# Adding a causal mask to attention scores: on VectorE in 32-bit floats, or as a bf16 product on TensorE

## The chip, the cores and the metric

The kernel runs on one core of one Trainium2 chip. The metric is the device time in microseconds of one execution. Five engines work side by side, each through its own queue in order: TensorE (PE in the profile, its weight loads PEld), VectorE (DVE), ScalarE (ACT), GpSimd (POOL) and SyncE (SP), which here issues the DMAs. TensorE writes its products to PSUM, which VectorE and ScalarE can read and write.

## The reference, cut to what matters

One decoder block over 1040 tokens (16 learned meta tokens ahead of 1024), model width 1024, all in 32-bit floats. After a norm and one input projection, 8 heads of 64 channels attend, beside a gated short convolution of 512 channels; both are normed by head, projected back, and a squared-ReLU MLP of width 4096 and a last norm follow. The attention adds a decay to the scores and masks the future:

```
s = einsum('bqhd,bkhd->bhqk', q_block, k) * scale
s = where(causal, s + cum[q] - cum[k], -1e30)
p = softmax(s);  out = einsum('bhqk,bkhd->bqhd', p, v)
```

A block of 128 queries sees 16 + 128 (i + 1) keys (i = 0 to 7); only the last 128 of them need the mask, a triangle.

## The kernel before

Products keep the precision of 32-bit floats by splitting each operand into a rounded part (type fp32r) and the rest: a ScalarE copy makes the first (`split`, L116), a VectorE or GpSimd subtract the second (`low`, L113), and three products are summed.

From about 111 us to 510 us the attention runs, as 64 slots: 8 heads of 8 query blocks (L696 to L739). A slot's work on its critical path is: `scores` (L513) writes 128 queries by 144 to 1040 keys into one PSUM tile `S` of three banks (one buffer), in one to three chunks, two products a chunk (L527, L528); behind the last chunk comes one more product, of an identity in bf16 with a bf16 mask of 0 and -1e30 (L530), onto the last 128 columns (132 for the longest block). VectorE takes the negated maximum of the rows (L533, `nm`), ScalarE the exponential with its sum (L537, `pr`). One slot later `transposed` (L541) turns `pr` by TensorE (L550) and splits it (`pth`, `ptl`, L116 and L113); behind every second slot `weighted` (L558) multiplies it with the values (L564 to L566).

What is independent of this fills TensorE's time. `fill` (L692) draws products from one list, so many nominal microseconds a slot (`QUOTA0`, then `QUOTA1`, four fifths of it behind the scores): first the rest of the input projections (`project`, L465), and from about 397 us, when these are used up, the convolution's half of the output projection (`out_conv`, L655). The latter loads its rows and weights through two buffers named `raw` (L589, L605), whose DMAs are ordered with TensorE's instructions, splits them (`yh`, `wa`, `wc`) and adds the result to the residual `h` (L669).

The order of TensorE's instructions in the attention is the order of the program (`pe`, L104). The other engines' queues are laid out by a planner, which estimates durations and takes what is ready, by priority; a queue once laid out is fixed. In the first part and after 514 us, most instructions of every engine are held in program order (`pin`, L109).

After the attention come the rest of the output projection with a norm (L851), and from about 592 us the two MLP products (L979, L1284), which TensorE works through with hardly a hole.

At the start (L80 to L89) GpSimd makes the identity `ident` in 32-bit floats, VectorE casts it to `identb`, and GpSimd makes `maskb` with a memset and a select.

Of the kernel before, what the change touches and what calls it, by code (L numbers as in the profile page):

```python
# [10 lines left out]

F32 = mybir.dt.float32
F32R = mybir.dt.float32r
BF16 = mybir.dt.bfloat16
AF = mybir.ActivationFunctionType
ALU = mybir.AluOpType
AX = mybir.AxisListType
# [3 lines left out]
P = 128  # L21
EPS = 1e-5
NEG = -1e30
# [18 lines left out]
def hymba_block(  # L42
# [5 lines left out]
    nc = tc.nc  # L48
# [6 lines left out]
    HD = 64  # L55
# [11 lines left out]
    KPAD = 4  # L67
# [6 lines left out]
        name=nc.get_next_instruction_name(), act_func_set_id=LN_EXP_SET, ins=[], outs=[]))  # L74

    const = ctx.enter_context(tc.tile_pool(name="const", bufs=1))
# [2 lines left out]

    ident = const.tile([P, P], F32, name="ident")  # L80
    make_identity(nc, ident)
    identb = const.tile([P, P], BF16, name="identb")
    nc.vector.tensor_copy(identb, ident)
    maskb = const.tile([P, P + KPAD], BF16, name="maskb")
    nc.gpsimd.memset(maskb, 0.0)
    nc.gpsimd.affine_select(
        out=maskb, in_=maskb, compare_op=ALU.is_ge, fill=NEG, base=0,
        pattern=[[-1, P + KPAD]], channel_multiplier=1,
    )  # L89
    bones = const.tile([P, P], F32R, name="bones")  # L90
# [13 lines left out]
    def pe(ins):  # L104
        return tc.keep_in_program_order(ins) if ORDERED[0] else ins
# [53 lines left out]
    def bank(tag):  # L159
        return pp.tile([P, 512], F32, name=tag, tag=tag, bufs=BANKS[tag])  # L160
# [140 lines left out]
    for g in range(0, NK, 4):  # L301
        ps = bank("tr")[:NH]
        w = 0
# [111 lines left out]
    def conv_groups(ct):  # L415
        st = {}
        p0 = NM - 2
        ch = chunks(p0, T + 2, 3)

        def evac_c(ps, t0, n):  # L420
            if not st:
                st["cu"] = page(st)
            nc.scalar.copy(st["cu"][:, t0 - p0:t0 - p0 + n], ps)

        def evac_u(ps, t0, n):
            cu = st["cu"][:, t0 - p0:t0 - p0 + n]
            nc.vector.tensor_tensor(out=cu, in0=ps, in1=cu, op=ALU.mult)

        def taps():
            cu = st["cu"]  # L430
            st["y"] = yc = page(st)[:, :T]
            nc.vector.tensor_scalar(yc, cu[:, 0:T], cw[:, 0, ct:ct + 1], None, op0=ALU.mult)
            for j in (1, 2):
                nc.vector.scalar_tensor_tensor(
                    out=yc, in0=cu[:, j:j + T], scalar=cw[:, j, ct:ct + 1], in1=yc, op0=ALU.mult, op1=ALU.add)

        def evac_b(ps, t0, n):
            s = st["y"][:, t0 - NM:t0 - NM + n]
            nc.vector.tensor_tensor(out=s, in0=ps, in1=s, op=ALU.mult)

        def norm():
            (a, b), (c, d) = head_norm(st["y"], NP + ct, 0), head_norm(st["y"], NP + ct, 1)

            def middle():
                b()
                c()

            pending.extend([a, middle, d])

        return [(CC + ct * P, ch, evac_c, None), (CU + ct * P, ch, evac_u, taps),  # L450
                (CB + ct * P, chunks(NM, T, 2), evac_b, norm)]
# [61 lines left out]
    def scores(i, st, s):  # L513

        qa, qb, ka, kb = st
        n = NM + P * (i + 1)
        nb = 2 * (i // 2) + 2
        qs = slice(i * P, (i + 1) * P)
        nch = -(-n // 512)
        pad = -n % (2 * nch)  # L520
        v = (n + pad) // nch
        w = max(v, 256)
        ps = pp.tile([P, 3, 512], F32, name="S", bufs=BANKS["S"])
        for c in range(nch):
            ks = slice(c * v, c * v + w)
            last = c == nch - 1
            pe(nc.tensor.matmul(ps[:, c, :w], qa[:, qs], ka[:, ks], start=True, stop=False))  # L527
            pe(nc.tensor.matmul(ps[:, c, :w], qb[:HD + 4, qs], kb[:HD + 4, ks], start=False, stop=not last))  # L528
            if last:
                pe(nc.tensor.matmul(ps[:, c, v - P - pad:v], identb, maskb[:, :P + pad], start=False, stop=True))  # L530
        ps = ps[:, :nch, :v]
        nm = small.tile([P, 1], F32, name="nm")
        nc.vector.tensor_reduce(nm, ps, axis=AX.XY, op=ALU.max, negate=True)  # L533
        pr = at.tile([P, L + KPAD], F32, name="pr", bufs=3)
        if n < nb * P:
            nc.gpsimd.memset(pr[:, n:nb * P], 0.0)
        nc.scalar.activation(  # L537
            pr[:, :n + pad].rearrange("p (a b) -> p a b", b=v), ps, AF.Exp, bias=nm, accum_out=s)
        return pr
# [137 lines left out]
    c = [conv_groups(ct) for ct in range(NC)]  # L677
# [22 lines left out]
    ORDERED[0] = True  # L700
    fill(START)
    pr = scores(0, st[0], sums[0][:, 0, 0:1])
    late = None
    for t, (h, i) in enumerate(slots):
# [8 lines left out]
        if t + 1 < len(slots):  # L713
            h1, i1 = slots[t + 1]
            p1, j1 = divmod(h1, 2)
            if p1 not in o:
                o[p1] = at.tile([P, T], F32, name="opair", bufs=2)
                sums[p1] = at.tile([P, NT, 2], F32, name="sums", bufs=2)
            pr = scores(i1, st[h1], sums[p1][:, i1, j1:j1 + 1])
# [588 lines left out]
    v = [vp.tile([P, HD2], F32, name=f"v{tt}") for tt in range(NH2)]  # L1308
# [136 lines left out]
```

## Time and profile before

| | |
|---|---|
| median of 3 runs | 1193.27 us (1193.04 to 1193.37) |
| the profiled execution | 1195.17 us, its span 1193.4 us |
| busy in the span, VectorE | 727.7 us (61%), 989 instructions |
| busy in the span, ScalarE | 544.5 us (46%), 911 instructions |
| busy in the span, GpSimd | 212.5 us (18%), 211 instructions |
| mean granted TensorE clock | 0.992 of full speed |
| chain that ended last, TensorE's share | 87% |

The span runs from the first instruction to the last; the execution's time is that and some 1.8 us around it. The profiled execution is one of its own and lies 1.9 us above the median. Matmul records overlap, since products are pipelined: what a product costs is read from starts, not from its duration. Idle time of an engine that doesn't set the end costs nothing.

### The profile page before, as it was taken

To read this page: it belongs to the slowest core of one execution; us is meant where nothing else is said; L and a number is where in the kernel's file an instruction comes from. 1 tells how busy PE (TensorE), PEld (TensorE's weight loads), DVE (VectorE), ACT (ScalarE), POOL (GpSimd) and SP (SyncE) were. 2 spreads that over 40 slices of the span, in tenths; PEclk is the share of its full clock that TensorE was granted. 3 is DMA by queue.
4 is the path that set the end of the run, shared out by engine and by line. 5 is a ranking of instruction groups with operands and counts; after the bars stand their busy time and mean duration, and the time that the engine had idled before them with its cause. 6 is when DMAs were issued, how large, how long until landed. Compare 5 with 4: busy or idle time off the path is not lost.

```text
span 1193.4 us, 15645 instructions
## 1 busy us (share of the span) xinstructions
PE 1155.6 (97%) x5969; PEld 982.8 (82%) x5969; DVE 727.7 (61%) x989; ACT 544.5 (46%) x911; POOL 212.5 (18%) x211
## 2 busy tenths in 40 slices
PE   6999999999999899998899999999999999999997
PEld 6988989899888677886788888888888888888886
DVE  7632354444454556659778866666665546985687
ACT  6522335453455555546444353444544433333444
POOL 3011123222221121201523431323100000000000
PEclk9999999999999899999999999999999999999999
DMA  8448241543332564265345445354479866522561
GB/s 249 148 140 246 72 89 41 144 136 77 80 105 77 193 172 159 98 212 175 107 133 194 159 133 193 109 183 140 152 248 344 289 201 222 159 89 71 185 238 71
DMA packets 120123, 185.92 MB, mean 156 GB/s; under 512 B 9552, under 2 KB 61776, under 8 KB 120048
## 3 DMA queue, kind: packets, MB, share of 16 engines
q1 hardware_dynamic: 120048, 184.92, 48.7%
q8 instruction: 47, 0.77, 0.3%
q14 instruction: 28, 0.23, 0.1%
HBM read 126.30 MB, written 58.59 MB: 155 GB/s over the span
## 4 chain that ended last, share of the span: by engine, by line
PE 87%; DVE 5%; DMA 3%; ACT 3%; issue 2%; DVEq 0%; ACTq 0%; SPq 0%
PE acc L1284 26%; PE acc L979 24%; PE mm L465 18%; PE tr L550 3%; PE mm L655 2%; PE wide L851 2%; PE mm L251 2%; PE S L251 1%; PE pv L564 1%; PE pv L565 1%; PE S L527 1%; PE S L528 1%; DMA raw<-y_conv 1%; DMA raw<-in_w_out_dram 1%; PE pv L566 1%
## 5 line engine op out<-in xcount | busy, mean ns | idle before, releaser
L1284 PE MATMUL acc<-w2h,a2l 128*128 128x512 f32 x440 | 171.2, 389 | 0.0
L1284 PE MATMUL acc<-w2h,a2h 128*128 128x512 f32 x440 | 171.2, 389 | 0.0
L1284 PE MATMUL acc<-w2l,a2h 128*128 128x512 f32 x440 | 171.2, 389 | 0.0
L465 PE MATMUL mm<-xh,wh 128*128 128x342 f32 (+3 forms) x416 | 145.0, 349 | 1.0 <-DVE vm L260 0.8
L465 PE MATMUL mm<-xh,wl 128*128 128x342 f32 (+3 forms) x416 | 144.8, 348 | 0.0
L465 PE MATMUL mm<-xl,wh 128*128 128x342 f32 (+3 forms) x416 | 144.7, 348 | 0.0
L116 ACT CAST a2h<-ar 128x1024 fp32r<-128x1024 f32 x54 | 56.8, 1052 | 147.5 <-PE acc L1284 83.2
L113 DVE TENSOR_TENSOR a2l<-ar,a2h 128x1024 fp32r<-128x1024 f32 x54 | 66.1, 1224 | 86.1 <-ACT a2h L116 86.1
L1284 PEld LDWEIGHTS acc<-w2h,a2l 128*128 128x128 f32 x440 | 82.6, 188 | 17.3
L1284 PEld LDWEIGHTS acc<-w2l,a2h 128*128 128x128 f32 x440 | 82.6, 188 | 17.2
L1284 PEld LDWEIGHTS acc<-w2h,a2h 128*128 128x128 f32 x440 | 82.6, 188 | 17.0
L465 PEld LDWEIGHTS mm<-xh,wh 128*128 128x128 f32 x416 | 78.5, 189 | 7.8 <-DVE vm L260 1.1
L465 PEld LDWEIGHTS mm<-xh,wl 128*128 128x128 f32 x416 | 78.5, 189 | 6.1
L465 PEld LDWEIGHTS mm<-xl,wh 128*128 128x128 f32 x416 | 78.6, 189 | 6.0
L113 DVE TENSOR_TENSOR ptl<-tr,pth 128x512 fp32r<-128x512 f32 (+1 forms) x96 | 56.1, 596 | 38.3 <-ACT pth L116 37.7
L113 POOL TENSOR_TENSOR wl<-wr,wh 128x512 fp32r<-128x512 f32 x40 | 53.4, 1355 | 116.0 <-ACT wh L116 99.1
L786 ACT ACTIVATE ac<-ac 128x1024 f32<-128x1024 f32 (+1 forms) x64 | 66.5, 1041 | 13.0 <-DVE ac L780 11.8
L537 ACT ACTIVATE pr<-S,nm 128x144 f32<-128x144 f32 (+3 forms) x64 | 48.5, 757 | 46.4 <-DVE nm L533 46.0
L116 ACT CAST pth<-tr 128x512 fp32r<-128x512 f32 (+1 forms) x96 | 47.7, 514 | 43.7 <-PE tr L550 31.4
L533 DVE TENSOR_REDUCE nm<-S 128x1 f32<-128x144 f32 (+3 forms) x64 | 49.3, 771 | 24.6 <-PE S L530 24.1
L780 DVE TENSOR_TENSOR ac<-acc,cv 128x512 f32<-128x512 f32 x61 | 41.7, 687 | 28.6 <-PE acc L979 28.4
L116 ACT CAST ws12h<-w1s 128x1024 fp32r<-128x1024 f32 x16 | 16.9, 1055 | 87.5 <-PE acc L979 84.3
(275 smaller groups left out, 2678.8 us busy)
## 6 DMA issues: line engine op xcount, KB each, us to landing
ar<-a_scr SPq DMA_DIRECT2D x54, 512.0 KB
w1r<-in_w_ff_dram SPq DMA_DIRECT2D x16, 1024.0 KB
a_scr<-ac SPq DMA_DIRECT2D x16, 1024.0 KB
a_scr<-sm SPq DMA_DIRECT2D x16, 768.0 KB
w<-in_w_ff_dram SPq DMA_DIRECT2D x24, 512.0 KB
wr<-in_w_in_dram SPq DMA_DIRECT2D x40, 256.0 KB
w2r<-in_w_ff_dram SPq DMA_DIRECT2D x16, 512.0 KB
k_scr<-pg SPq DMA_DIRECT2D x8, 520.0 KB
```

The source lines that it names most:

```text
L113: pin((eng or nc.vector).tensor_tensor(out=lo, in0=src, in1=r32(hi), op=ALU.subtract))
L116: pin(nc.scalar.copy(hi, src))
L251: pin(nc.tensor.matmul(ps[half], lhs, w_[:, k, f0:f0 + fn], start=k == 0 and a == 0, stop=k == KD - 1 and a == len(terms) - 1))
L465: pe(nc.tensor.matmul(ps, x_[:, k], y_[:, k, ts], start=k == 0 and a == 0, stop=k == KD - 1 and a == 2))
L533: nc.vector.tensor_reduce(nm, ps, axis=AX.XY, op=ALU.max, negate=True)
L537: nc.scalar.activation(pr[:, :n + pad].rearrange("p (a b) -> p a b", b=v), ps, AF.Exp, bias=nm, accum_out=s)
L550: pe(nc.tensor.transpose(ps[:, jj], pr[:, kt * P:(kt + 1) * P], ident))
L655: pe(nc.tensor.matmul(ps, y_[:, k], w_[:, cs], start=k == 0 and a == 0, stop=k == NC - 1 and a == 2))
L780: pin(eng.tensor_tensor(out=out, in0=a, in1=b, op=ALU.add))
L786: pin(nc.scalar.activation(out, src, func, **more))
L979: pe(nc.tensor.matmul(ps, w[w_][:, k], m[m_][:, k], start=k == a == 0, stop=k == HK - 1 and a == 2))
L1284: pe(nc.tensor.matmul(banks[tt], w[w_][:, k, tt * P:(tt + 1) * P], m[m_][:, k], start=first and f == k == a == 0, stop=last and f == len(f ...
```

## The change

The bf16 identity and mask go, and the mask is kept in 32-bit floats. In `scores`, the last chunk's second product ends the accumulation like the others, the third product is gone, and VectorE adds the mask to the last 128 (or 132) columns in PSUM, in place, before the maximum.

```diff
-    identb = const.tile([P, P], BF16, name="identb")
-    nc.vector.tensor_copy(identb, ident)
-    maskb = const.tile([P, P + KPAD], BF16, name="maskb")
-    nc.gpsimd.memset(maskb, 0.0)
+    mask = const.tile([P, P + KPAD], F32, name="mask")
+    nc.gpsimd.memset(mask, 0.0)
     nc.gpsimd.affine_select(
-        out=maskb, in_=maskb, compare_op=ALU.is_ge, fill=NEG, base=0,
+        out=mask, in_=mask, compare_op=ALU.is_ge, fill=NEG, base=0,
         pattern=[[-1, P + KPAD]], channel_multiplier=1,
     )
...
         for c in range(nch):
             ks = slice(c * v, c * v + w)
-            last = c == nch - 1
             pe(nc.tensor.matmul(ps[:, c, :w], qa[:, qs], ka[:, ks], start=True, stop=False))
-            pe(nc.tensor.matmul(ps[:, c, :w], qb[:HD + 4, qs], kb[:HD + 4, ks], start=False, stop=not last))
-            if last:
-                pe(nc.tensor.matmul(ps[:, c, v - P - pad:v], identb, maskb[:, :P + pad], start=False, stop=True))
+            pe(nc.tensor.matmul(ps[:, c, :w], qb[:HD + 4, qs], kb[:HD + 4, ks], start=False, stop=True))
+        end = ps[:, nch - 1, v - P - pad:v]
+        nc.vector.tensor_tensor(out=end, in0=end, in1=mask[:, :P + pad], op=ALU.add)
         ps = ps[:, :nch, :v]
```

## Rows read from the trace of the kernel before

**Rows 1.** The page, busy time: engine, us, share of the span, instructions.
```profile
PE 1155.6 (97%) x5969; PEld 982.8 (82%) x5969; DVE 727.7 (61%) x989; ACT 544.5 (46%) x911; POOL 212.5 (18%) x211
...
```

**Rows 2.** Stretches: us, engines' busy us (instructions), TensorE's clock, DMA share, GB/s.
```profile
111.00:397.00 286.00, 283.99 (x1740) 255.59 (x1739) 124.94 (x204) 131.47 (x288) 66.23 (x81) 1.00 0.35 98
397.00:467.00 70.00, 60.15 (x334) 47.21 (x333) 44.17 (x72) 41.24 (x88) 14.09 (x20) 0.95 0.59 177
467.00:514.00 47.00, 47.00 (x266) 38.82 (x267) 25.88 (x47) 23.34 (x53) 8.72 (x10) 0.96 0.38 125
...
592.00:1150.00 558.00, 558.00 (x2463) 462.05 (x2462) 378.72 (x408) 237.66 (x261) 86.17 (x60) 1.00 0.54 181
```

**Rows 3.** Weight loads' waits, 111-396, then 396-515 us: total us, times, longest.
```profile
PEld tr L550 <- ACT pr L537: 1.6, 2, 1.3
...
PEld tr L550 <- ACT pr L537: 9.5, 8, 2.6
```

**Rows 4.** Chain that ended last, 396 to 468 us: start, us, what.
```profile
414.14 0.89 DVE nm L533
...
430.20 4.85 DMA raw<-in_w_out_dram
...
435.73 1.30 DVE wa L113
...
451.81 0.46 DVE nm L533
```

**Rows 5.** Mask products in 113-397, 398-467, 467-515 us: durations, first and last start.
```profile
L530 PE MATMUL S<-maskb,identb x42: 230/231/233, 113.4 to 396.5; 128*128 128x128 bf16 x37, 128*128 128x132 bf16 x5
...
L530 PE MATMUL S<-maskb,identb x13: 230/231/233, 399.1 to 461.8; 128*128 128x128 bf16 x11, 128*128 128x132 bf16 x2
...
L530 PE MATMUL S<-maskb,identb x8: 230/231/232, 468.2 to 498.6; 128*128 128x128 bf16 x7, 128*128 128x132 bf16 x1
```

**Rows 6.** TensorE in order of time around one mask: start us, us, instruction.
```profile
241.11 0.31 PE L527 MATMUL S<-ka,qa 128*128 128x328 f32 x1
241.26 0.31 PE L528 MATMUL S<-kb,qb 68*128 68x328 f32 x1
241.41 0.23 PE L530 MATMUL S<-maskb,identb 128*128 128x128 bf16 x1
241.45 0.48 PE L465 MATMUL mm<-xh,wl 128*128 128x512 f32 x1
241.77 0.39 PE L465 MATMUL mm<-xh,wh 128*128 128x512 f32 x1
242.00 0.39 PE L465 MATMUL mm<-xl,wh 128*128 128x512 f32 x1
```

**Rows 7.** VectorE by shape (busy, mean ns, idle before), then tile S (min/median/max ns).
```profile
L113 DVE TENSOR_TENSOR ptl<-tr,pth 128x512 fp32r<-128x512 f32 x64 | 43.8, 687 | 38.2 <-ACT pth L116 37.7
...
L113 DVE TENSOR_TENSOR tail<-tr,tail 16x128 fp32r<-16x128 f32 x32 | 9.0, 280 | 32.4 <-ACT tail L116 32.1
...
L113 DVE TENSOR_TENSOR vt<-S,vt 128x256 fp32r<-128x256 f32 x8 | 3.4, 421 | 11.0 <-ACT vt L116 11.0
...
L263 DVE TENSOR_TENSOR zt<-S,bfb x4: 153/156/156, 32.5 to 68.6; 128x8 f32<-128x8 f32 x4
```

**Rows 8.** VectorE in order of time: a dependent pair, then an independent one.
```profile
6.16 0.22 DVE L121 SCALAR_TENSOR_TENSOR rs_t<-rs_r,rs_v 128x1 f32<-128x1 f32 x1 [0.41 <-ACT rs_r L131]
6.41 0.16 DVE L122 SCALAR_TENSOR_TENSOR rs_t<-rs_t,rs_r 128x1 f32<-128x1 f32 x1
...
241.02 0.75 DVE L370 SCALAR_TENSOR_TENSOR n_y<-pg,og,n_sq 128x512 f32<-128x512 f32 x1 [1.23 <-ACT n_sq L368]
...
241.69 0.83 DVE L533 TENSOR_REDUCE nm<-S 128x1 f32<-128x656 f32 x1
```

**Rows 9.** VectorE in order of time at the start; in brackets its idle time before.
```profile
2.35 0.96 DVE L83 CAST identb<-ident 128x128 bf16<-128x128 f32 x1
...
5.59 0.15 DVE L130 TENSOR_SCALAR rs_v<-ss 128x1 f32<-128x1 f32 x1 [2.29 <-ACT xn L210]
```

More of the change, by code (lines that the diff above doesn't have):

```diff
@@ L13 @@
 F32R = mybir.dt.float32r
-BF16 = mybir.dt.bfloat16
 AF = mybir.ActivationFunctionType
```

## The prediction

> **What bounds the kernel now.** I read the page first: TensorE is busy for 1155.6 us of a span of 1193.4 us [rows 1], so the question is where its 37.8 idle us lie and where a saved product is saved time. Busy time by stretch answers that [rows 2]. From 111 to 397 us, where scores alternate with the projections that fill TensorE's time, TensorE is busy for 284.0 of 286 us with the granted clock at 1.00: this stretch is as long as TensorE's list of products. From 397 to 467 us, where the filler has become the output projection, it is busy for only 60.2 of 70 us and the clock's mean is 0.95. From 467 to 514 us the records cover the stretch again. From 592 to 1150 us TensorE is busy all the time, and the planner's freedom is small there, so what the attention gains or loses reaches the end of the kernel.
>
> The waits come next, because the change lengthens one path: scores, maximum (VectorE), exponential (ScalarE), transposes (TensorE). In the first stretch TensorE's weight load for the transposes waits for the exponential only 2 times, 1.6 us in all; from 396 us on it waits 8 times, 9.5 us in all [rows 3]. So the path has slack nearly everywhere before 396 us and little behind it. The chain of waits shows what sets the time behind it: a ring of loads into the two `raw` buffers, a DMA (4.85 us in the row), a ScalarE cast, VectorE subtracts that free the buffer (1.30 us for two), and the next DMA; at four places between 397 and 467 us the chain passes through the maximum L533, of which the first and the last are shown [rows 4].
>
> **The mask product that goes.** All 64 score tiles have one: 42 start between 113 and 397 us, 13 between 398 and 467, 8 between 467 and 514 [rows 5], and the first of all stands at 111.5 us. Its record lasts 0.230 us, but records overlap; what counts is how much later the following products start. In the close look [rows 6] the mask starts at 241.41, the first filler product at 241.45, the second at 241.77 and the third at 242.00. The last pitch, 0.23 us, is the undisturbed one for 512 columns. From the mask to the second filler product it is 0.36 us; without the mask the first filler would start at 241.41 and the second 0.23 us later, so the mask costs 0.36 - 0.23 = 0.13 us, which I take for all. The bounds are 0.04 us (the pitch mask to first filler alone) and 0.230 us (the record). Taking a product out of a queue in order can't lengthen that queue, so nothing lies below zero.
>
> *What each would make:* 42 x 0.13 = 5.5 us in the first stretch; by the bounds 1.7 to 9.7 us. In the last stretch 8 x 0.13 = 1.0 us. In the middle stretch I count nothing for the 13 products, since TensorE waits there anyway.
>
> The array itself needs less for 128 columns: 0.23 x 128/512 = 0.058 us by the 512-column pitch. The rest, some 0.07 us, I read as the filler's weight load that the short product doesn't cover. The Trainium skill ("TensorE: Matmul & The Clock Gate", Back-to-back issue gap) gives an isolated product the columns over the clock plus 2.5 ns, which is about 56 ns for 128 columns; by that the first stretch would give only some 2.4 us. The trace differs with 0.13 us, and I go by it; that other outcome is the first rival.
>
> **The add that comes.** 64 VectorE adds of 128 rows by 128 columns (132 in 8 of them), one input and the output in PSUM, the mask in SBUF. No row shows VectorE writing PSUM. Rows that read PSUM [rows 7]: 128x8 takes 0.155 us, 16x128 takes 0.280, 128x256 takes 0.421. Ends 0.155 and 0.421; I take 0.280, the row with the same number of columns, since the time of a row grows with columns (0.421 at 256, 0.687 at 512). It isn't zero or less: an instruction is added and none on VectorE goes in the loop.
>
> The Trainium skill's rule against such a step ("Advanced Engine Details and Errata", TRN2 Errata) is that memory latency stands bare between VectorE instructions, and that tiles of 512 or 1024 elements keep its share small. The rows agree: 256 columns fewer save only 0.266 us of 0.687, so about 0.155 us of the add is fixed.
>
> The maximum reads what the add writes, so it can't overlap it. Independent neighbours overlap: the maximum at 241.69 starts 0.08 us before the end of the instruction ahead of it (241.02 + 0.75). A dependent pair shows a hole: 6.16 + 0.22 = 6.38, and the next starts at 6.41, 0.03 us later [rows 8]. The path therefore grows by 0.28 + 0.03 = 0.31 us on VectorE. It starts earlier, though: the last score product now ends it. By the close look that product ends at 241.26 + 0.31 = 241.57 and the mask at 241.64, so 0.07 us come back where TensorE's product released VectorE. Net 0.24 us there, 0.31 us where VectorE's own queue is the cause.
>
> The add takes the place in VectorE's queue where the maximum stood and waits for TensorE as that did; behind it stand the maximum, then the subtracts `ptl`, `wa`, `wc`, `h`, for which the probability x value products and the ring wait. ScalarE's queue stands behind the exponential in the same way. The PSUM tile S is still freed by the exponential, so no wait moves there.
>
> *What lies beside other work:* in the first stretch VectorE is busy for 124.9 of 286 us [rows 2]; 42 x 0.31 = 13 us more fit. Two tiles wait on the path already (the very first, and one near 299 us): 2 x 0.24 = 0.5 us lost. In the middle stretch the chain passes four maxima: 4 x 0.31 = 1.2 us lost. (If all 13 counted it would be 4.0, at the bounds of the add 2.4 to 5.9 with the hole.) In the last stretch one of the eight waits lies: 0.24 us lost.
>
> **The rest.** The identity's cast to bf16 goes: 0.96 us of VectorE at 2.35 us, but VectorE then sits idle for 2.29 us until 5.59 [rows 9], so nothing. The mask is built in 32-bit floats on GpSimd, off every path until 111 us. The constants grow by 8 bytes a partition, 520 to 528; no row prices that, and I take nothing. The instructions that are not held in order are placed again by the planner; the one wait it could make or remove is of the size of those seen, 1 to 2 us either way, and I take nothing but keep it in the range.
>
> **Sum**, against the profiled execution of 1195.17 us (span 1193.4 and 1.8 around it): -5.5 + 0.5 + 1.2 - 1.0 + 0.2 = -4.6 us, so about 1190.6 us for an execution like that. The profiled one is 1.9 us above the median of the runs, 1193.27; the same difference on the median gives **1188.7 us**.
>
> **Rivals.**
>
> *The mask costs only its columns.* If the hole behind it is not the mask's but the change from scores to filler, which stays, each product gives 0.058 us: 42 x 0.058 = 2.4, plus 8 x 0.058 = 0.5, less the same 1.9 lost: -1.0 us, 1192.3. For it: the first filler product's record is longer (0.48 against 0.39 us) behind the mask, and no trace shows it without. Against it: where score products of one tile follow each other, at 241.11 and 241.26, the pitch is 0.15 us for 328 columns, which is 0.23 x 328/512: no hole [rows 6]. This is also the way in which the change would do less for TensorE than it says. Chance 0.13.
>
> *The middle stretch eats most of it.* All 13 adds land on the ring or on the chain, 4.0 us in place of 1.2: -4.6 + 2.8 = -1.8 us, 1191.5. For it: TensorE waits in 7 of these tiles. Against it: half of the ring's time is DMA. Chance 0.10.
>
> *Slower: the ring slips a turn.* Place: 397 to 467 us. The subtract `wa` or the cast behind it stands behind the add and the maximum, a buffer comes free after the issue that should follow it, and the load ordered behind it lands after the products that need it. Price: the 4.0 us of all adds, and two waits of the size of the longest there, 2.6 us [rows 3], so 5.2 us, together 9.2. Against gains of 5.5 + 1.0 - 0.7 = 5.8 that is +3.4 us, 1196.7. It decides from losses of 5.8 + 2.4 = 8.2 us on. For it: VectorE is busy for 44 of 70 us, the clock falls below 1.00 there, and a new placement can open such a wait. Against it: the extra time in a turn is a tenth of its DMA. Chance 0.18.
>
> **Chances and range.** The forecast, faster by 2.4 to 6.8 us, has 0.55. A larger gain, where also the middle stretch keeps its masks' time, 64 x 0.13 = 8.3 us, has 0.04. One measurement can tell this kernel from no change by about 0.2%, 2.4 us. Faster: 0.55 + 0.04 = 0.59; within: 0.13 + 0.10 = 0.23; slower: 0.18. The forecast's own range is 1186.5 to 1190.9. The range for 8 in 10 begins at 1185.0, the full gain, and ends at 1196.0, which leaves out the greater part of the slower case.
>
> **What would show it.** Steps: no product at the place of the mask, and the pitch from the last score product to the filler undisturbed (else the first rival); the adds at 0.28 us and the maximum 0.03 us behind them; the start of the 42nd tile some 5 us earlier than 396.5; waits of the transposes for the exponential before 396 us still few; from there to 514 us a stretch longer by up to 0.5 us; from 592 us on the same length as now. The prediction is wrong if TensorE starts to wait in the first stretch, if the stretch from 397 to 467 us grows by more than 3 us, or if the stretch behind 592 us doesn't keep the gain.

## The result and the profile after

The change makes the kernel slower: 1200.99 us, median of 4 runs (1200.05 to 1202.58), against 1193.32 us for the kernel before on the same chip, a ratio of 1.0070 [1.0056, 1.0084], 8.4 us of 1193.3. I forecast 1188.7 us and a faster kernel. The profiled execution of after took 1200.05 us (span 1198.2), that of before 1195.17. These two differ by less than the 8.4 us, because the one of before lies 1.9 us above its kernel's median and the one of after 0.9 below: the traces show 4.8 us of the loss. Executions of one kernel spread over several us, so a difference of a few us between two traces is not by itself a difference between two kernels.

The page of after, busy time of each engine:

```profile
PE 1148.3 (96%) x5905; PEld 982.1 (82%) x5905; DVE 743.0 (62%) x1052; ACT 543.9 (45%) x911; POOL 214.0 (18%) x211
```

TensorE is busy for 7.3 us less than in [rows 1] and has 64 products fewer, VectorE for 15.3 us more. What was meant to happen to the amounts of work did happen. The span grew by 4.8 us all the same, so TensorE's idle time grew by 12.1 us, from 37.8 to 49.9 (1198.2 - 1148.3). Busy time by stretch, as in [rows 2], says where:

```profile
111.00:397.00 286.00, 282.28 (x1718) 258.06 (x1716) 136.60 (x253) 133.09 (x294) 67.46 (x82) 1.00 0.35 100
397.00:470.00 73.00, 57.28 (x297) 46.25 (x297) 43.05 (x78) 38.29 (x81) 13.14 (x18) 0.91 0.53 158
470.00:520.00 50.00, 45.94 (x259) 37.48 (x258) 29.04 (x57) 24.09 (x55) 9.45 (x12) 1.00 0.37 123
597.00:1155.00 558.00, 558.00 (x2463) 462.40 (x2462) 383.08 (x411) 237.92 (x261) 86.97 (x60) 1.00 0.54 181
```

The first stretch is still TensorE's, and so is the last, as long as before. In the 123 us between 397 and 520 TensorE is idle for 15.7 + 4.1 = 19.8 us. Before, it was idle for 9.9 us of 397 to 467 and for none of the 47 behind. Which path it waits for is read from the waits of the weight loads between 396 and 515 us, to be set beside the second of [rows 3] (total us, times, longest):

```profile
PEld tr L546 <- ACT pr L533: 20.2, 12, 3.3
```

20.2 us against 9.5, and 12 waits against 8: TensorE waits for the exponential. One maximum later by 0.3 us per tile can't make that; 21 tiles x 0.3 = 6.3 us would be all of it. ScalarE's own waits for TensorE in the same stretch give the first hint, here of after:

```profile
ACT tail L113 <- PE tr L551: 10.9, 6, 3.1
```

and here of before:

```profile
ACT tail L116 <- PE tr L555: 1.4, 2, 0.7
```

ScalarE, which must run the exponential, stands 10.9 us at a cast of `tail` that waits for TensorE; before it stood there for 1.4. ScalarE works off its queue in order (the 55th tile, below, shows it), so what stands behind such a cast waits as well. This is a hint only: ScalarE's waits at the casts `yh` for their DMAs fell at the same time, from 9.3 to 5.1 us. The start of the first score product of a tile (read from the trace, us) dates the loss:

| tile | before | after | after - before |
|---|---|---|---|
| the 43rd | 396.03 | 392.16 | -3.87 |
| the 55th | 455.47 | 458.42 | +2.95 |
| the 57th | 467.85 | 472.31 | +4.46 |
| the 64th, the last | 497.59 | 504.05 | +6.46 |
| first product behind the attention | 513.84 | 520.15 | +6.31 |

So 3.9 us were gained before 396 us and 10.3 us were lost between there and the last tile. At the first product of the tile `acc`, with which the stretch of the MLP begins, 4.8 us are left (592.42 and 597.23), and they reach the end: the two profiled spans differ by the same 4.8. The 55th tile shows how. In the trace of after, in order of time (start us, us, engine, instruction, in brackets idle time before it and what ended it):

```profile
460.99 0.28 DVE L526 TENSOR_TENSOR S<-S,mask 128x128 f32<-128x128 f32 x1
461.19 0.41 DVE L110 TENSOR_TENSOR ptl<-tr,pth 128x256 fp32r<-128x256 f32 x1
...
461.52 1.09 DVE L529 TENSOR_REDUCE nm<-S 128x1 f32<-128x912 f32 x1
461.52 0.26 ACT L113 CAST tail<-tr 16x128 fp32r<-16x128 f32 x1 [1.49 <-PE tr L551]
...
463.13 0.62 ACT L113 CAST wa<-raw 128x512 fp32r<-128x512 f32 x1 [1.36 <-DMA raw<-in_w_out_dram]
463.66 1.01 ACT L533 ACTIVATE pr<-S,nm 128x912 f32<-128x912 f32 x1
...
464.82 1.97 PE L546 MATMUL tr<-ident,pr 128*128 128x128 f32 x8 [2.87 <-ACT pr L533]
```

The maximum doesn't follow the add at once: a `ptl` subtract stands between (0.25 us). The next step is longer. The maximum ends at 462.61, and the exponential starts at 463.66, because a cast `wa` stands ahead of it in ScalarE's queue and waits until 463.13 for a DMA. TensorE waits 2.87 us. Over the last 22 tiles it is the other way round: between add and maximum lie 12.5 us in all, from the maximum to the exponential 6.9, hardly other than in before (7.0). TensorE's own queue, apart from the mask products, has the same order in both kernels; the queues of VectorE, ScalarE, GpSimd and SyncE do not: the planner laid them out again. Compared position by position by names and shapes, without the adds, VectorE's queue differs in 106 positions, ScalarE's in 85, GpSimd's in 4 and SyncE's in 5.

### The profile page after: what moved, and what is told of

It is laid out like the page before. It is cut to its first block, busy times and chain, and to the rows that moved or that the text cites. A ratio compares the mean times of both kernels' runs of the same rounds, so it can differ in the third digit from the quotient of the medians.

```text
span 1198.2 us, 15577 instructions
## 1 busy us (share of the span) xinstructions
PE 1148.3 (96%) x5905; PEld 982.1 (82%) x5905; DVE 743.0 (62%) x1052; ACT 543.9 (45%) x911; POOL 214.0 (18%) x211
## 4 chain that ended last, share of the span: by engine, by line
PE 86%; DVE 5%; ACT 3%; DMA 3%; issue 2%; POOL 0%; ACTq 0%; SPq 0%; DVEq 0%
PE acc L1280 25%; PE acc L975 24%; PE mm L462 18%; PE tr L546 3%; PE wide L847 2%; PE mm L651 2%; PE mm L248 2%; PE S L248 1%; PE S L524 1%; PE S L523 1%; PE pv L560 1%; PE pv L561 1%; DMA raw<-in_w_out_dram 1%; ACT pr L533 1%; DMA raw<-y_conv 1%
## 5 line engine op out<-in xcount | busy, mean ns | idle before, releaser
L782 ACT ACTIVATE ac<-ac 128x1024 f32<-128x1024 f32 (+1 forms) x64 | 66.6, 1042 | 13.4 <-DVE ac L776 12.4
L546 PE MATMUL tr<-ident,pr 128*128 128x128 f32 x320 | 48.3, 282 | 19.8 <-ACT pr L533 16.8
L546 PEld LDWEIGHTS tr<-ident,pr 128*128 128x128 f32 x320 | 38.7, 144 | 30.2 <-ACT pr L533 23.5
```

Of the source, the lines that this page charges most:

```text
L546: pe(nc.tensor.transpose(ps[:, jj], pr[:, kt * P:(kt + 1) * P], ident))
L782: pin(nc.scalar.activation(out, src, func, **more))
```

## The experiments

Each kernel was timed in five rounds against the kernel before on the same chip. "Us" below is the ratio less one, times 1193.3; the chip is not the same for all of them. The name in brackets is the run's.

**Order held, add kept** (add_before_order). The instructions of the attention's four other queues get order-only links (no waits), so that they stand as in before, with each add directly ahead of its maximum:

```
+QUEUES = {"DVE": [...], "Activation": [...], "Pool": [...], "SP": [...]}
+    traced = len(nc.cur_bb.bb.instructions)       # ahead of fill(START)
...
+    for e, order in QUEUES.items():
+        for a, b in zip(order, order[1:]):
+            tc.add_manual_dep(queues[e][b], queues[e][a].name, ...)   # order only
```

> The changed kernel, but from 111 to 514 us the queues of VectorE, ScalarE, GpSimd and SyncE are laid out in the order of the kernel before, each add directly ahead of its maximum. Theory A (the planner's new order costs the time, above all the work that it put between an add and its maximum): the loss goes and the saving of the first stretch stays, 1189 to 1192 us. Theory B (the add's own 0.3 us on the path costs it, whatever the order): 1198 to 1201 us. Theory C (TensorE, running ahead by 4 us, falls out of step with the loads behind 397 us): also 1198 to 1201 us.

Measured 0.9978 [0.9965, 0.9991], median 1191.40 us: 2.6 us faster than before, with the add in all 64 tiles. The order makes the loss, 11.0 us of it (1.0070 against 0.9978); theory A holds, and the theories by which the add does it in any order fall. The tile of the fence above, in its trace:

```profile
457.97 0.29 DVE L578 TENSOR_TENSOR S<-S,mask 128x128 f32<-128x128 f32 x1
458.29 1.11 DVE L581 TENSOR_REDUCE nm<-S 128x1 f32<-128x912 f32 x1
...
459.50 1.02 ACT L585 ACTIVATE pr<-S,nm 128x912 f32<-128x912 f32 x1 [0.17 <-DVE nm L581]
...
460.66 0.33 PE L598 MATMUL tr<-ident,pr 128*128 128x128 f32 x1 [0.81 <-ACT pr L585]
```

Add, maximum (0.03 us behind it) and exponential (0.10 us behind) follow each other, and TensorE waits 0.81 us in place of 2.87.

**Order of after, product kept** (pe_after_order). The reverse: the kernel before, mask on TensorE, no add, laid out in after's order.

> The kernel before, with its mask product on TensorE and no add, but with the four queues laid out in the order of the changed kernel. Theory A: the loss comes without the add, 1200 to 1205 us (the saving of 4 us in the first stretch is missing). Theory B: the order does little, 1192 to 1195 us. Theory C: nothing runs ahead, 1192 to 1195 us.

Measured 1.0112 [1.0093, 1.0130], 1207.59 us, 2.6 us beyond the range of theory A. The order alone, without any add, costs 13.4 us. Its weight loads' waits in 396 to 515 us are nearly those of after:

```profile
PEld tr L599 <- ACT pr L586: 19.0, 13, 3.3
```

**Mask left out, order of before** (no_mask_before_order). The lines with `end` and the add are removed; the scores aren't masked.

> No mask at all (it is left out, so later keys are seen), the queues in the order of the kernel before. It gives what the 64 products cost on TensorE. All but C: 42 + 8 products that count at 0.12 us, 1187 us, down to 1185.5 if the middle ones count too. Theory C: it falls out of step without any add, 1194 to 1198 us. The difference to the add in the same order is the add's own price: some 2 us by A, some 12 us by B.

Measured 0.9957 [0.9940, 0.9974], 1188.54 us. That is 1.5 us above the 1187 expected. All mask products are worth 5.1 us, and the adds cost 0.9978 - 0.9957 = 2.5 us in this order (2.7 by the means of the runs of the two, timed on one chip, with a 95% interval of some 1.0 to 4.4). In its trace the 43rd tile starts at 391.00, 5.03 us earlier than in before: 0.12 us for each of 42 products. (The spans of the two profiled executions differ by 8.8 us, but this one lies 2.2 us below its kernel's median and that of before 1.9 above.)

**Maximum tied to its add** (add_tight). After's order, but each maximum is moved right behind its add.

```
-    'DVE': [..., add, ptl, max, ...]
+    'DVE': [..., add, max, ptl, ...]        # wherever something stood between
```

> The changed kernel in its own order, but each maximum is moved up directly behind its add. Theory A in its narrow form (the work between add and maximum is what costs): 1190 to 1195 us. Theory A in its wide form (other places of the new order cost it): 1197 to 1201 us. Theory B and C: 1199 to 1201 us.

Measured 1.0043 [1.0028, 1.0057], 1198.85 us: of 8.4 us, 3.3 come back. The narrow form of theory A falls, the wide one holds. Over the last 22 tiles the time between the end of the add and the start of the maximum falls from 12.5 to 0.8 us, but that from the end of the maximum to the start of the exponential grows from 6.9 to 13.1: the wait goes over to ScalarE's queue.

**Exponential ahead of the casts that stood in its way** (path_first). As before it, and 13 exponentials are moved ahead of casts of `tail`, `opair`, `wa` and `yh`.

```
-    'Activation': [..., tail, exp, ...]
+    'Activation': [..., exp, tail, ...]
```

> The changed kernel in its own order, with each maximum directly behind its add, and 13 exponentials between 395 and 502 us moved ahead of the casts (tail, opair, wa, yh) that stood ahead of them in ScalarE's queue. Theory D (the new order holds the path scores - add - maximum - exponential behind other work in both queues, and that is the loss): 1190 to 1194 us. Theory E (other places of the new order cost it: the ring of raw loads, SyncE's queue): 1197 to 1200 us, as with the maximum alone moved.

Measured 1.0029 [1.0014, 1.0043], 1196.54 us. Both ranges are missed: some 1.6 us come back, with intervals that overlap, and 6 stay behind add_before_order. ScalarE's waits at `tail` have all but gone, from 11.6 us in add_tight to 1.2, so these waits were no measure of the loss. In its trace (an execution 4.3 us above the kernel's median) the wait has only gone on:

```profile
461.71 0.62 ACT L165 CAST wa<-raw 128x512 fp32r<-128x512 f32 x1 [2.16 <-DMA raw<-in_w_out_dram]
462.35 0.86 ACT L165 CAST pth<-tr 128x512 fp32r<-128x512 f32 x2
462.97 0.69 DVE L162 TENSOR_TENSOR ptl<-tr,pth 128x512 fp32r<-128x512 f32 x1
...
463.71 0.28 PE L603 MATMUL tr<-ident,pr 128*16 128x128 f32 x1 [2.12 <-DVE ptl L162]
```

The exponential is through, but the cast `pth` of the transposed probabilities stands behind the cast `wa`, which waits for a DMA; `ptl` follows it, and TensorE waits 2.12 us for a buffer.

**VectorE's queue alone back in before's order** (dve_order_alone), the three others in after's:

> The changed kernel with VectorE's queue in the order of the kernel before, the adds directly ahead of their maxima, and the other queues in its own order. Theory D: ScalarE's queue still holds the exponential behind other casts, so only a part comes back, 1194 to 1199 us. Theory E: with the other queues unchanged, little comes back, 1198 to 1201 us. If VectorE's order alone were the cause: 1191 to 1192 us.

Measured 1.0079 [1.0058, 1.0100], 1203.51 us, above all three ranges: nothing comes back, and it is 4.3 us slower by the ratios than add_tight, whose other queues stand in the same order. One queue put back alone is no better than none; it is the four queues together that fit or don't. (The converse, VectorE's queue in after's order and the others in before's, wasn't run.)

**Those casts and subtracts as well** (path_and_ring). As path_first, and `pth` casts ahead of `wa` and `yh` casts (16 places), `ptl`, add and maximum ahead of `wa` subtracts (13 places).

> As path_first, and from the 43rd tile on the pth casts are moved ahead of the wa and yh casts that stood directly ahead of them in ScalarE's queue (16 places passed), and on VectorE the ptl subtracts, adds and maxima ahead of wa subtracts (13 places). Theory D2 (the same cause, with the casts of the transposes as further victims: work of the path queued behind casts that wait for a DMA): the rest of the loss goes, 1191 to 1193.5 us. Theory E (SyncE's order or the ring itself): it stays at 1195 to 1198 us, or gets worse because the ring's casts come later.

Measured 1.0009 [0.9997, 1.0021], 1193.95 us: 2.4 us more come back, again with intervals that overlap a little, to 0.5 us beyond the upper end of what theory D2 gave. Against after, the three kinds of swap together are clear of the noise.

**One exponential more** (path_all), that of the 56th tile, which in the run ahead waited 5.2 us (461.68 to 466.88) behind two casts `wa` and a cast `yh`:

> As path_and_ring (1194.0 us), with one exponential more, that of tile 56 near 466.9 us, moved ahead of the two wa casts and the yh cast that held it for 5.2 us in that trace. Theory D2: the transposes behind it waited 5.5 us there, TensorE fell back by 3.8 us at this tile; with it gone the order of the kernel before is nothing special any more, 1190 to 1192 us. Theory E (some rest of the new order, SyncE's queue with it): 1193 to 1195 us.

Measured 1.0012 [1.0001, 1.0024], 1195.17 us: no gain, a miss for theory D2 and, within 0.2 us, what theory E gave. Its trace at that tile:

```profile
462.86 0.69 DVE L162 TENSOR_TENSOR wa<-raw,wa 128x512 fp32r<-128x512 f32 x1 [2.01 <-ACT wa L165]
463.47 0.68 DVE L717 TENSOR_TENSOR h<-mm,h 128x512 f32<-128x512 f32 x1
464.07 0.68 DVE L162 TENSOR_TENSOR ptl<-tr,pth 128x512 fp32r<-128x512 f32 x1
464.81 0.66 PE L598 MATMUL tr<-ident,pr 128*128 128x128 f32 x4 [1.78 <-DVE ptl L162]
...
466.15 0.62 ACT L165 CAST wa<-raw 128x512 fp32r<-128x512 f32 x1 [3.33 <-DMA raw<-in_w_out_dram]
```

Now `ptl` stands behind a subtract `wa`, which waits 2.01 us for its cast, and TensorE waits 1.78 us behind `ptl`. The exponential runs 5.8 us earlier than in path_and_ring (461.10 against 466.88) and the 57th tile starts 4.6 us earlier (465.22 against 469.77), but of that the 59th has only 0.8 left (477.88 against 478.69): the next step of the path stands behind an instruction of the ring of loads. And the ring itself has become slower. The load of `raw` issued at 456.34 is cast only at 462.21, 5.87 us later, because a cast `pth` and the exponential stand ahead of this cast; in add_before_order the same load and cast lie 2.66 us apart (459.76 and 462.42). SyncE's next load waits for the subtract behind the cast, between 430 and 475 us here:

```profile
SPq L637 <- DVE wa L162: 6.0, 2, 4.6
```

and in add_before_order:

```profile
SPq L637 <- DVE wa L162: 0.5, 1, 0.5
```

**The other way round** (tail_first). add_before_order, with 4 exponentials put behind the `tail` cast next to them:

> The converse: the add with all queues in the order of the kernel before (1191.4 us), but for 4 exponentials (near 415, 447, 485 and 494 us) that change places with the tail cast behind them in ScalarE's queue, as the planner has them in the changed kernel. Theory D: an exponential then waits until TensorE has worked through four fifths of its filler and reached the tail's transpose; by the waits of the changed kernel 1 to 3 us each, of which slack takes a half: 1194 to 1198 us. Theory E: 1190.5 to 1192.5 us.

Measured 0.9995 [0.9983, 1.0007], 1192.52 us: 2.0 us slower by the ratios than without the swaps, but the intervals overlap. It lies at the upper end of theory E's range and below that of theory D, so D's price is not borne out. ScalarE stands 7.0 us at `tail` there (1.3 in add_before_order). The direction fits, but a proof it is not.

**Add where there is slack, product where there is none** (split_by_stage). The adds for the first 43 tiles, in which TensorE's list is the bound, and the bf16 product for the 21 behind, in the planner's own order. Against the kernel before (the mask stays in bf16, and these adds read it so; they take 0.30 us as well):

```
-            last = c == nch - 1
+            last = c == nch - 1 and "op" in after
...
+        if "op" not in after:
+            end = ps[:, nch - 1, v - P - pad:v]
+            nc.vector.tensor_tensor(out=end, in0=end, in1=maskb[:, :P + pad], op=ALU.add)
```

> The add on VectorE for the 43 tiles of the first stretch, the product on TensorE for the 21 behind it; the planner lays out the queues. The saving of the first stretch, 3.7 us by the traces, stays, and the later path is that of the kernel before: 1189 to 1191 us if the planner leaves the later queues as they were; with a new order there, anything up to 1200 us.

Measured 0.9958 [0.9941, 0.9975], 1188.31 us: 5.0 us faster than before, 0.7 beyond the range given for unchanged later queues, and faster than after. Its weight loads wait less than in [rows 3]:

```profile
PEld tr L553 <- ACT pr L540: 7.3, 6, 2.0
```

**The same in before's order** (split_before_order):

> The same division, the four queues laid out as in the kernel before, each add directly ahead of its maximum. By all theories but E the best: 1193.4 - 3.7 = 1189.7 us, 1188.5 to 1190.5.

Measured 0.9961 [0.9946, 0.9976], 1188.27 us, no different. The traces say which order split_by_stage has: up to the 43rd tile all four queues stand as in after, behind it as in before but for three exchanges of neighbours, two on VectorE and one on ScalarE. So after's new order of the first stretch costs nothing that can be measured; what costs is, by difference, its order behind the 43rd tile, in the stretch where the path has no slack (no run has that late order alone). With no add among the last tiles the planner did not make that order.

The two changes against each other, and the repairs, in us against before:

| | order of before | order of after |
|---|---|---|
| mask product (TensorE) | 0 | +13.4 |
| add (VectorE) | -2.6 | +8.4 |

After +8.4; maximum tied +5.1; exponentials moved +3.5; `pth`, `ptl` moved +1.1; one exponential more +1.4; the whole order of before -2.6.

## Why the prediction was wrong

**The mask product: right.** I took 0.13 us for each; the kernel without masks gives 0.12. Between the scores and the filler the pitch of after is undisturbed, where [rows 6] had 0.36 us from the mask to the second filler product. TensorE of after:

```profile
239.57 0.31 PE L523 MATMUL S<-ka,qa 128*128 128x328 f32 x1
239.73 0.31 PE L524 MATMUL S<-kb,qb 68*128 68x328 f32 x1
239.88 0.40 PE L462 MATMUL mm<-xh,wl 128*128 128x512 f32 x1
240.11 0.40 PE L462 MATMUL mm<-xh,wh 128*128 128x512 f32 x1
```

0.15 us from score to filler, then 0.23. The rival by which a mask costs its columns alone, 0.058 us, falls: by it 42 products give 2.4 us, and 5.03 were seen.

**The add: right.** I took 0.28 us, from a row of another shape. All 64, min/median/max in ns:

```profile
L526 DVE TENSOR_TENSOR S<-S,mask x64: 283/299/304, 112.2 to 505.3; 128x128 f32<-128x128 f32 x56, 128x132 f32<-128x132 f32 x8
```

0.30 us, and the maximum 0.03 us behind it where nothing stands between.

**The gain before 396 us: nearly.** I looked for some 5 us at the 43rd tile (the prediction calls it the 42nd, but a first mask stands ahead of the 42 counted); 3.87 came in after and 3.63 in add_before_order. Without masks and adds 5.03 came, so the adds cost 1.2 to 1.4 us in this stretch, where I had 0.5.

**What the adds cost on the path: about right, at an unchanged order.** 0.5 + 1.2 + 0.2 = 1.9 us forecast, 2.5 measured (no_mask_before_order against add_before_order), some 1.0 to 4.4 with the noise. The whole sum, -6.5 + 1.9 = -4.6, stands against -5.1 + 2.5 = -2.6 for add_before_order: just inside the forecast's bounds of 2.4 to 6.8, with an interval of 1.1 to 4.2. No run of the changed kernel in its own order came near it.

**The MLP keeps what the attention brings: right.** From 597 us TensorE is busy throughout, with the same 2463 products in 558 us.

**The step that failed** is one sentence: "The instructions that are not held in order are placed again by the planner; the one wait it could make or remove is of the size of those seen, 1 to 2 us either way, and I take nothing but keep it in the range." It is not one wait, and not 1 to 2 us. The planner laid out four queues again, and that costs 11.0 us with the add (1.0070 against 0.9978) and 13.4 without it. In 48 of 64 tiles something stands between add and maximum; exponentials stand behind casts that wait for TensorE's later transposes or for DMAs. From the end of a tile's last product in `S` to the start of the exponential the last 22 tiles of before need 35.2 us together, those of add_before_order 42.8, those of after 54.5. The 11.7 us between the last two are as much as what after has more between add and maximum (12.5 against 0.8); the other parts cancel. Moving the maximum up alone brings back only 3.3 us, because the wait goes over to ScalarE. I had worked out that this path has no slack behind 396 us, and then priced only its length and not what else is queued on the engines that it runs through.

**The slower rival** (the ring slips a turn, 1196.7 us, 0.18) had the place and the sign. Two loads of `raw` that lie 3.2 us apart in before (463.54 and 466.71) lie 6.1 apart in after (464.50 and 470.62), and by the start of the 57th tile 8.3 of the 10.3 us are lost, more than the 3 us which the prediction names as a sign of being wrong. The rival's price was two waits; there are four more, and longer ones: TensorE's waits for the exponential grew by 20.2 - 9.5 = 10.7 us. Nor is the add what makes the ring slip: in pe_after_order, slower still, the same two loads lie 6.2 us apart (469.43 and 475.65).

**What stays open.** The three kinds of swap bring back 7.3 of 11.0 us (path_and_ring). Of the other 3.7, path_all shows where: its 57th tile starts 2.6 us earlier than that of before (465.22 against 467.85), its 59th 0.8 us later (477.88 against 477.05). Between them the ring of loads has fallen back: the instructions that were moved ahead stand ahead of its casts, and SyncE waits up to 4.6 us for a subtract. That fits theory E, but no run puts the ring's casts back and keeps the rest. SyncE's queue, which in after differs from before in only five positions (near 440 and 470 us), was changed only together with the other queues. The mean granted clock of 397 to 470 us is 0.91 in after, 0.94 in before and 0.93 in add_before_order. Had TensorE worked all through the stretch, 0.02 of 73 us would be some 1.5 us, an estimate from these means; so the clock carries a small part of the 11.0 us at most. Whether TensorE's waits make it lower or it adds to them, no run tells apart.

## What to carry to other kernels

Where a planner lays out queues, one instruction more is priced by two numbers, its own time and that of the new order; run the change in the old order and the old kernel in the new one before you judge it. On engines that work off their queues in order, ask of each instruction of a tight path what stands ahead of it and what that waits for. But a wait found in this way is not yet a price: ScalarE's waits at `tail` fell by 10.4 us from add_tight to path_first, and 1.6 us came back. Put work on the engine that has slack in that stage, and keep the order of the stage that has none: split by stage, the change gives 0.9958 [0.9941, 0.9975], where everywhere it gives 1.0070 [1.0056, 1.0084]. Most of that is order; in before's order the two give 0.9961 [0.9946, 0.9976] and 0.9978 [0.9965, 0.9991], 2.0 us apart with intervals that overlap.

## What the runs showed of the hardware

A bf16 product of 128 columns between 32-bit products costs the stream 0.12 us (5.03 us over 42), though the columns at the pitch of its neighbours are 0.058. VectorE adds 128 by 128 32-bit floats in place in PSUM in 0.30 us, and a reduction that reads the sum starts 0.03 us behind. The Trainium skill ("VectorE: DVE Perf Modes", The TRN2 errata) gives for a 32-bit add of two tensors the columns plus 151, over 0.96 GHz: an estimate of 291 ns for 128 columns, which the 299 ns agree with, though here one input and the output lie in PSUM.

ScalarE does not go round an instruction that waits. In after the maximum of the 55th tile ends at 462.61 us and its exponential starts at 463.66, with ScalarE idle until a DMA lands at 463.13 and a cast of 0.62 us run first; with another order of the same instructions (add_before_order) the hole is 0.10 us. The Trainium skill ("PSUM — Partial Sum Buffer", Engine vs sequencer instructions) states that the queues of ScalarE, VectorE and GpSimd are strictly first in, first out; these rows agree for ScalarE.
